# Products over a head's 64 channels on all 128 rows, in a two-layer hybrid decoder trunk

## The chip, the core and the metric

The kernel runs on one core of a Trainium2 chip. The metric is the device time of one execution in microseconds, the median of the runs. The kernel before takes 2547.66 us (median of 3 runs, 2547.12 to 2550.92). The engines are named as the profile names them: PE is TensorE's products and PEld its weight loads, DVE is VectorE, ACT ScalarE, POOL GpSimd, SP the engine that issues the transfers.

## The reference

Two layers over 256 tokens of 2048 channels, all in float32. A layer projects the normalized tokens once and hands the columns to three branches, whose results are gated and summed:

```python
h = rmsnorm(x, pre_norm[i])
pa, pb, pc, pg = split(h @ w_in[i])
y_a = mamba2_branch(pa, ...)      # state space, 16 heads of 64 channels
y_b = rwkv7_branch(pb, ...)       # delta rule, 16 heads of 64 channels
y_c = dsa_branch(pc, ...)         # sparse attention, 16 heads of 64 channels
merged = sum of sigmoid(gate_i) * (y_i @ w_branch_i)
x = x + rmsnorm(merged @ w_out[i], post_norm[i])
```

Three places contract over the 64 channels of one head. In branch B a low-rank product of 64 (decay and a) and, for each head, the Gram products of keys and key directions with key directions and receptances, 128 tokens at a time. In branch C the index scores (each of 16 index heads' queries with one shared key) and the attention logits:

```python
logits_idx = einsum('bqhd,bsd->bqhs', iqb, ik)          # 64 channels
score = einsum('bqh,bqhs->bqs', iwb, relu(logits_idx))  # then the top 64 keys of each query
logits = einsum('bqgrd,bqkgd->bqgrk', qg, ks)           # 64 channels
```

## The kernel before

Products that have to be exact to about float32 are made of two parts. An operand is split into a high part (rounded to `float32r`, which PE takes in one pass) and a low part (the rest), and a product is high x high + high x low + low x high. Over 128 channels that is three products (`acc`). Over a head's 64 channels the kernel has two helpers that need only two products. `stack` puts the high part of an operand on the head's 64 partitions and its low part on the other 64. `twice` puts the high part of the other operand on both halves and its low part into a separate tile, on the head's own half alone. `acc2` then issues a product over all 128 rows (high x high and low x high in one), and a second one over the head's 64 rows only (high x low):

```python
def acc2(self, out, w, x, lo, h, first=True, last=True):
    hs = self.HALF[h]
    self.mm(out, w, x, first, False)
    self.mm(out, w[hs], lo[hs], False, last)
```

`acc2` is called in `rwkv_prep` (the low-rank products, 2 for each of 8 channel blocks, and in `gram` 8 for each), in `index_scores` (one for each of 16 heads) and in `attend` (2 for each of 8 blocks). In the last two it takes the second 128 tokens' queries with all 256 keys. The first 128 tokens, which see 128 keys, take a plain float32 product there, `self.mm(pl[:, 0:128], ...)`, over 64 rows. A plain float32 product appears in the profile as two records.

Around this, weights stream through SP into `wraw`, ACT rounds them to `whi`, DVE (now and then POOL) subtracts to `wlo`, 512 columns at a time, and PE runs three products of 128x256 for each block of weights into a `psg` bank. Work of the branches is written as generators that are advanced between the products (`pump`), and its results lie in `psa` banks. Nothing is issued in the order in which it is written: every instruction is noted, and `Program.issue` replays them on a cost model of the core, giving each engine its most pressing ready instruction. All instructions are therefore issued from one line, L418. Each engine then runs its own list in order. The model's cost of a product depends on its type and columns; it has no term for the number of rows.

A layer runs the projections in the order `BCBBBBCCCCBBBBCCCCBBBBCCCCBBBBCAAAAAAAAAAAA`, then 48 merge steps (`c`, `b`, `a`, 16 each), then the output projection. Layer 1 has its merge from about 808 to 1249 us, layer 2 from about 2072 to 2503 us.

Of the kernel before, what the change touches and what calls it, by code (L numbers as in the profile page):

```python
# [37 lines left out]
# rotary order of a head's 64 channels: both of a pair lie in one quadrant of 32 partitions  # L38
# [8 lines left out]
def in_blocks():  # L47
    """Columns of w_in by block of 128 (-1 pads with zeros)."""
    ar = np.arange
    b = {}  # L50
# [21 lines left out]
# a layer's projections: units of two blocks, and the order in which the branches take turns  # L72
# [12 lines left out]
def plan():  # L85
    """The order in which a layer's weights come: (kind, which), in chunks of 128 x 1024."""
    p = []
    at = {k: iter(u) for k, u in UNITS.items()}
    for b in ORDER:
        u = next(at[b])  # L90
        p += [("cv", None)] if u == "cv" else [("br", w[1:]) if w[0] == "br" else ("in", w) for w in u]
    p += [("out", q) for q in range(4)]
    return p
# [14 lines left out]
def consts():  # L108
# [9 lines left out]
    # rows 8 i + q of a unit matrix, on the partitions 16 q to 16 q + 15  # L118
# [5 lines left out]
def pack(inp):  # L124
    """Layout of the inputs for the chip: copies only."""
# [77 lines left out]
class Program:  # L203
    """A sequential program of instructions, issued in the order in which a model of the core would run them.

    Instructions are noted as the trunk calls for them. issue() then gives each engine, whenever it is free, the most
    pressing instruction whose operands are there, so that no engine's queue waits on a result that comes late."""

# [21 lines left out]
    def tile(self, t, tag, bufs):  # L230
        """A tile of a tag takes one of its slots from its first access to its last."""
        of = self.tags.setdefault(tag, (bufs, []))
        assert of[0] == bufs
        self.tiles[t.tensor.name] = [tag, len(of[1]), 0, 0.0]
        of[1].append(t.tensor.name)
        return t

    @staticmethod
    def region(ap):
        """Partitions and columns that an operand may touch."""  # L240
# [14 lines left out]
    def note(self, eng, op, f, a, k):  # L255
# [6 lines left out]
        for aps, writes in ((r, False), (w, True)):  # L262
            for ap in aps:
# [8 lines left out]
                if writes or ap.space == bass.MemoryType.PSUM:  # L272
                    # of two engines that read a bank, one waits for the other
# [15 lines left out]
    def cost(eng, op, out, r, k):  # L289
        """Time on the engine, and after that until the result is there."""  # L290
# [24 lines left out]
    def issue(self, tc):  # L315
# [14 lines left out]
        # slots: of each tag, the tiles that are not yet dead, in order  # L330
# [102 lines left out]
urgent = ranked(0)      # frees the products' banks  # L433
critical = ranked(-1)   # all else waits for it
# [4 lines left out]
class Trunk:  # L439
# [66 lines left out]
    def rsqrt(self, x):  # L506
        """x (SBUF, > 0) -> x ** -0.5 in a new tile, to float32's accuracy."""
# [4 lines left out]
        # a first guess from the exponent, then y (15 - 10 x y^2 + 3 (x y^2)^2) / 8 (3/8 of it left out),  # L512
        # then y (3 - x y^2) / 2 (with that 3/8 put in)
# [24 lines left out]

    def rope_tables(self):
        """cos and signed sin of positions * frequency, reduced to a turn exactly by 12-bit parts."""  # L540
# [16 lines left out]
        # 1/(2 pi) = 0.15915494309189533576888376337251436...  # L557
# [20 lines left out]
        for dst, off in ((self.sin, 0.0), (self.cos, 0.25)):  # L578
# [4 lines left out]
            # a turn's fraction in [-1/2, 1/2]; the margin keeps the product within the table's range  # L583
# [31 lines left out]
    def fetch(self):  # L615
        """Load the next 128 x 1024 of weights."""
        l, n = divmod(self.nraw, self.wst.shape[1])
        if l < NL:
            # a layer's last ones come early, in room that the branches have left
# [6 lines left out]
    def prepare(self):  # L626
        """Weights of the products ahead, 128 x 512 at a time, each as an exact sum of two parts of 12 bits."""
        self.prog.rank, was = 1, self.prog.rank
        while len(self.ready) <= LA and (self.raw or self.nraw < NL * self.wst.shape[1]):
# [17 lines left out]
            # the last ones of a layer are kept for a second use, as quarters  # L647
# [18 lines left out]
    def parts(self, a):  # L666
        """a [128, 256] as (high, low)"""
# [5 lines left out]
    # Products over 64 channels, two at a time: the other 64 partitions add the low part's.  # L673
    HALF = (slice(0, 64), slice(64, 128))

    def stack(self, p, a, h):
        """p: on half h of the partitions the high part of a, on the other half the low part."""
# [4 lines left out]
    def twice(self, p, lo, a, h):  # L682
        """p: on both halves the high part of a, which lies on half h; lo, there: the low part."""
# [5 lines left out]
    def acc2(self, out, w, x, lo, h, first=True, last=True):  # L689
        """out += w.T @ x, w from stack, x and lo from twice."""  # L690
        hs = self.HALF[h]
        self.mm(out, w, x, first, False)
        self.mm(out, w[hs], lo[hs], False, last)

    def total(self, out, sel, x, first=True, last=True):
        """Sums over the partitions that sel (zeros and ones) names."""
# [4 lines left out]
    def acc(self, out, w, x, first, last):  # L701
        """out += w.T @ x, w and x as (high, low)."""
# [4 lines left out]
    def block(self, l, out, x, nch):  # L707
        """out [128, S] = a block of 128 columns of weights times x (pair of [128, 8 nch, S])."""
# [15 lines left out]
    def split(self, src, hi, lo, scale=None):  # L724
        """hi + lo = src (times a power of two), exactly."""
# [8 lines left out]
    def residual(self, src):  # L734
        """The residual stream, tokens on partitions: two tiles [128, DM]."""
# [6 lines left out]
    def square(self, ss, x):  # L742
        """ss [128, 1] = sum of squares of x [128, n] / DM"""
        self.s.activation(self.t2(512)[:, :x.shape[1]], x, AF.Square, scale=DM ** -0.5, accum_out=ss)

    def rstd(self, ss):
# [3 lines left out]
        # as rsqrt, in fewer steps  # L750
# [9 lines left out]
    def sums(self, n):  # L760
        """Room for n parts of a mean square, and 1e-6."""
# [5 lines left out]
    def prenorm(self, x, ss, u):  # L767
        """h as (high, low), channels on partitions."""
# [3 lines left out]
        # u: room for the scaled tokens  # L772
# [25 lines left out]
    def rope(self, outs, x, n):  # L798
        """x [P, n, S] (PSUM or SBUF) rotated, into each of outs."""
# [11 lines left out]
    def silu2(self, out, x_ps):  # L811
        """2 * silu(x)"""
# [10 lines left out]
    def misc_work(self, m1):  # L823
        v, s = self.v, self.s
        yield
        # index key: layer norm over its 64 channels, then rotary
# [19 lines left out]
        # tokens onto partitions  # L846
# [10 lines left out]
        # softplus(x) = max(x, 0) + log1p(u), u = exp(-|x|); log1p(u) = 2 atanh(u / (2 + u))  # L857
# [26 lines left out]
        # rows of it for all partitions to read  # L884
# [12 lines left out]
    @urgent  # L897
    def mix(self, x_ps, i):
        """Token shift: x (1 - mu) + mu x[t - 1]"""
# [5 lines left out]
    def rwkv_lora(self, x_ps):  # L905
        t = self.mix(x_ps, 0)
        self.s.activation(t[0:64], t[0:64], AF.Tanh)
        self.tw = [self.t1(dt=F32R) for _ in range(3)]
        for h in range(2):
            self.twice(self.tw[h], self.tw[2], t[self.HALF[h]], h)  # L910

    def rwkv_prep(self, Q, j, rm, km, vm):
# [14 lines left out]
        for h, p in enumerate((pl0, pl1)):  # L927
            self.stack(w2[:, h, :], w2r[self.HALF[h]], h)
            self.acc2(p[:, :S], w2[:, h, :], self.tw[h], self.tw[2], h)
# [6 lines left out]
        # normalized key direction  # L936
# [4 lines left out]
        # log decay = -KAP (1 + thw); its running sum per chunk, measured from the chunk's middle  # L941
# [13 lines left out]
        # k2 = k (1 + (a - 1) k_a), a = (1 + al) / 2  # L955
# [9 lines left out]
        # of a chunk: key directions for the deltas, receptances for the outputs  # L965
# [8 lines left out]
        # bonus  # L974
# [5 lines left out]
        As = [[self.t1(dt=F32R).rearrange("p (a t) -> p a t", a=2) for _ in range(3)] for _ in range(2)]  # L980
        for c in range(2):
            for h in range(2):
                self.twice(As[c][h], As[c][2], AR[c][self.HALF[h]], h)
# [594 lines left out]
```

## Time and profile before

| what | value |
|---|---|
| median of 3 runs | 2547.66 us (2547.12 to 2550.92) |
| profiled execution, span from first to last instruction | 2533.4 us |
| PE busy | 2447.7 us, 97% |
| DVE, ACT, POOL busy | 69%, 54%, 42% |
| mean granted clock of PE | 0.982 |
| moved by DMA | 407.71 MB, 161 GB/s |

The profiled execution's own time isn't listed apart from its span; the span is 14.3 us below the median of the runs. In the rows, `psg` is a bank of the large products, `psa` a bank of the branches', `t` any of the ring's tiles, `hh` and `hl` the high and low parts of the normalized tokens. A form such as 64\*128 is rows x columns of PE that a product uses, and the size behind it what it streams. A timeline's row merges neighbours with the same names: its start is the first one's, its length runs to the last one's end, and its form is the first one's.

### The profile page before, as it was taken

The page shows a single profiled execution, that of the slowest core. Times are in us where ns is not written, and L with a number is a line of the kernel's source. Part 1 is how long each engine was busy: PE and PEld are TensorE (multiplying, and loading weights), DVE is VectorE, ACT ScalarE, POOL GpSimd, SP SyncE. Part 2 cuts the span into 40 slices and gives each one's busy share as a digit, 9 for nine tenths or more (in the row PEclk, how much of TensorE's full clock was granted, in tenths as well). Part 3 has the DMA queues.
Part 4 walks back from the last instruction along what each step waited for, and adds up shares of the span by engine and source line. Part 5 has one row for each costly group of instructions (what it writes and reads, how often), then busy time and mean ns, then how long its engine had stood idle before and what let it go on. Part 6 is the DMA issues. An engine that isn't in the chain of part 4 may idle for free.

```text
span 2533.4 us, 50627 instructions
## 1 busy us (share of the span) xinstructions
PE 2447.7 (97%) x18750; PEld 2250.0 (89%) x18750; DVE 1750.5 (69%) x3466; ACT 1374.8 (54%) x2882; POOL 1059.9 (42%) x1726
## 2 busy tenths in 40 slices
PE   8999999999999999999989999999999999999998
PEld 7878888888889999999888888888888899999987
DVE  8856787678987565556576676786779865655565
ACT  6745555656544554545566554565565445544453
POOL 2556776577851000101134586686777500100001
PEclk9999999999999999999999998999999999999999
DMA  5363453625634565555543634536364445755563
GB/s 192 135 147 125 132 165 111 150 100 159 180 127 152 188 234 195 189 188 201 192 138 135 156 134 133 147 127 151 113 161 156 136 158 187 244 183 186 189 209 134
DMA packets 175192, 407.71 MB, mean 161 GB/s; under 512 B 73504, under 2 KB 76512, under 8 KB 173664
## 3 DMA queue, kind: packets, MB, share of 16 engines
q1 hardware_dynamic: 174944, 404.48, 50.6%
q8 instruction: 147, 2.41, 0.4%
q14 instruction: 101, 0.83, 0.1%
HBM read 395.99 MB, written 8.42 MB: 160 GB/s over the span
## 4 chain that ended last, share of the span: by engine, by line
PE 78%; DVE 9%; POOL 6%; issue 3%; DMA 3%; ACT 1%; SPq 0%; POOLq 0%; DVEq 0%; ACTq 0%
PE psg L418 65%; PE psa L418 13%; POOL t L418 6%; DVE t L418 5%; DVE wlo L418 3%; DMA d<-diag 1%; DMA wraw<-in_wst 1%; ACT t L418 1%; ACT whi L418 0%; DVE yb L418 0%; DMA t<-diag 0%; DVE n_x L418 0%; DMA yb<-in_x 0%; POOL ya L418 0%; SPq L418 0%
## 5 line engine op out<-in xcount | busy, mean ns | idle before, releaser
L418 DVE TENSOR_TENSOR wlo<-wraw,whi 128x512 fp32r<-128x512 f32 x1352 | 1023.7, 759 | 612.0 <-ACT whi L418 579.5
L418 ACT ACTIVATE whi<-wraw 128x512 fp32r<-128x512 f32 x1361 | 855.8, 631 | 831.0 <-PE psg L418 745.7
L418 PE MATMUL psg<-hh,wlo 128*128 128x256 f32 x4224 | 1206.3, 286 | 4.6 <-DVE wlo L418 4.3
L418 PE MATMUL psg<-hh,whi 128*128 128x256 f32 x4224 | 1207.8, 286 | 0.0
L418 PE MATMUL psg<-hl,whi 128*128 128x256 f32 x4224 | 1202.3, 285 | 1.0 <-DVE hl L418 1.0
L418 PEld LDWEIGHTS psg<-hh,wlo 128*128 128x128 f32 x4224 | 803.7, 190 | 20.3 <-DVE wlo L418 7.0
L418 PEld LDWEIGHTS psg<-hh,whi 128*128 128x128 f32 x4224 | 805.0, 191 | 14.8 <-issue 7.1
L418 PEld LDWEIGHTS psg<-hl,whi 128*128 128x128 f32 x4224 | 804.8, 191 | 14.2 <-issue 5.7
L418 POOL TENSOR_TENSOR t<-t,t 64x256 fp32r<-64x256 f32 (+30 forms) x822 | 547.2, 672 | 360.9 <-ACT t L418 253.0
L418 POOL TENSOR_TENSOR b_nm<-b_nm,t 128x256 f32<-128x256 f32 x64 | 48.6, 759 | 664.8 <-DVE t L418 657.1
L418 POOL TENSOR_TENSOR t<-t,d 128x63 f32<-128x63 f32 (+42 forms) x504 | 257.9, 513 | 62.8 <-DMA d<-diag 22.0
L418 PE MATMUL psg<-t,whi 128*128 128x256 f32 x1536 | 282.3, 283 | 0.0
L418 PEld LDWEIGHTS psg<-t,whi 128*128 128x128 f32 x1536 | 239.2, 191 | 0.9 <-issue 0.5
L418 ACT ACTIVATE t<-t 64x256 fp32r<-64x256 f32 (+4 forms) x420 | 173.8, 418 | 91.7 <-DVE t L418 75.8
L418 PE MATMUL psg<-t,wlo 128*128 128x256 f32 x768 | 217.6, 283 | 0.0
L418 PE MATMUL psa<-t,t 128*64 128x128 f32 (+4 forms) x800 | 191.6, 338 | 12.1 <-ACT t L418 6.4
L418 PEld LDWEIGHTS psa<-t,t 128*64 128x64 f32 (+2 forms) x800 | 112.4, 168 | 71.3 <-ACT t L418 8.2
L418 PEld LDWEIGHTS psg<-t,wlo 128*128 128x128 f32 x768 | 147.1, 192 | 0.4 <-issue 0.2
L418 ACT ACTIVATE t<-psa 128x256 f32<-128x256 f32 (+4 forms) x206 | 79.7, 396 | 105.7 <-PE psa L418 102.7
L418 PE MATMUL psg<-whi,hh 128*128 128x512 f32 (+1 forms) x268 | 98.5, 368 | 0.0
L418 PE MATMUL psg<-wlo,hh 128*128 128x512 f32 (+1 forms) x268 | 97.9, 365 | 0.0
L418 PE MATMUL psg<-whi,hl 128*128 128x512 f32 (+1 forms) x268 | 97.2, 365 | 0.0
(236 smaller groups left out, 2227.2 us busy)
## 6 DMA issues: line engine op xcount, KB each, us to landing
wraw<-in_wst SPq DMA_DIRECT2D x688, 512.0 KB, 3.3
d<-diag SPq DMA_DIRECT2D x64, 128.0 KB, 6.3
d<-diag SPq DMA_DIRECT2D x64, 64.0 KB, 5.4
t<-diag SPq DMA_DIRECT2D x16, 256.0 KB, 4.3
d<-in_wst SPq DMA_DIRECT2D x8, 512.0 KB, 4.6
ya<-in_x SPq DMA_DIRECT2D x8, 256.0 KB, 4.8
yb<-in_x SPq DMA_DIRECT2D x8, 256.0 KB, 6.2
t<-in_cst SPq DMA_DIRECT2D x8, 256.0 KB, 3.7
```

Of the source, the lines that this page charges most:

```text
L418: ops[i][2](*ops[i][3], **ops[i][4])
```

## The change

The low part is given 128 rows. A new tile `zl` holds 14 slots of 256 columns, set to zero once by POOL; `twice` writes a low part onto the head's half of a slot, and the other half stays zero. `acc2` then names all rows for both products. The low part of the index key already lay on both halves, where the 64 rows of the stack's low part now meet it too. The first tokens' float32 products in `index_scores` and `attend` become calls of `acc2` on 128 columns. For that the stacks hold all 256 tokens: `index_scores` makes a stack of its own for each head, just before its products, where it made two for four heads; `attend` has one tile for each head instead of one for both. The DMA scratch is reduced, which makes room for `zl`. Comments are left out of the new file.

```diff
+        self.zl = self.T([128, 14, S], "zl", dt=F32R)
+        self.g.memset(self.zl.bitcast(F32), 0.0)
...
-    def acc2(self, out, w, x, lo, h, first=True, last=True):
-        hs = self.HALF[h]
+    def acc2(self, out, w, x, lo, first=True, last=True):
         self.mm(out, w, x, first, False)
-        self.mm(out, w[hs], lo[hs], False, last)
+        self.mm(out, w, lo, False, last)
...
-        self.tw = [self.t1(dt=F32R) for _ in range(3)]
+        self.tw = [self.t1(dt=F32R) for _ in range(2)]
         for h in range(2):
-            self.twice(self.tw[h], self.tw[2], t[self.HALF[h]], h)
+            self.twice(self.tw[h], self.zl[:, 8 + h, :], t[self.HALF[h]], h)
...
-        As = [[self.t1(dt=F32R).rearrange("p (a t) -> p a t", a=2) for _ in range(3)] for _ in range(2)]
+        As = [[self.t1(dt=F32R).rearrange("p (a t) -> p a t", a=2) for _ in range(2)] for _ in range(2)]
+        Al = [[self.zl[:, 4 * jj + 2 * c + h, :].rearrange("p (a t) -> p a t", a=2) for h in range(2)] for c in range(2)]
...
-                    self.acc2(pG[:, c], M[h][:, ts], As[c][h], As[c][2], h)
+                    self.acc2(pG[:, c], M[h][:, ts], As[c][h], Al[c][h])
...
     def index_scores(self, iq, n):
-        iqs = [self.t1(dt=F32R).rearrange("p (c t) -> p c t", c=2) for _ in range(2)]
-        for h in range(2):
-            self.stack(iqs[h], iq[self.HALF[h], :, 128:256], h)
         for h in range(4):
-            yield
             hd = 4 * n + h
-            hs = slice(64 * (h % 2), 64 * (h % 2) + 64)
+            iqs = self.t1(dt=F32R)
+            self.stack(iqs, iq[self.HALF[h % 2], h // 2, :], h % 2)
+            yield
             pl = self.P()
-            self.mm(pl[:, 0:128], iq[hs, h // 2, 0:128], self.ik[hs, 0, 0:128])
-            self.acc2(pl[:, 128:384], iqs[h % 2][:, h // 2, :], self.iks[0], self.iks[1], h % 2)
+            self.acc2(pl[:, 0:128], iqs[:, 0:128], *[a[:, 0:128] for a in self.iks])
+            self.acc2(pl[:, 128:384], iqs[:, 128:256], *self.iks)
...
     def attend(self, j, q):
-        qs = self.t1(dt=F32R).rearrange("p (h t) -> p h t", h=2)
+        qs = [self.t1(dt=F32R) for _ in range(2)]
         for h in range(2):
-            self.stack(qs[:, h, :], q[self.HALF[h], 128:256], h)
+            self.stack(qs[h], q[self.HALF[h]], h)
...
-            self.mm(pl[:, 0:128], q[hs, 0:128], self.ck[hs, gp, 0:128])
-            self.acc2(pl[:, 128:384], qs[:, hb, :], self.cks[gp][hb], self.cks[gp][2], hb)
+            ks = self.cks[gp][hb], self.zl[:, 10 + 2 * gp + hb, :]
+            self.acc2(pl[:, 0:128], qs[hb][:, 0:128], *[a[:, 0:128] for a in ks])
+            self.acc2(pl[:, 128:384], qs[hb][:, 128:256], *ks)
...
-    nc = _bacc.Bacc("TRN2", target_bir_lowering=False, num_devices=1)
+    nc = _bacc.Bacc("TRN2", target_bir_lowering=False, num_devices=1, dynamic_dma_scratch_size=1024)
```

The order of issue is computed anew from the changed instructions. Three places show it. In a row stands what is written, then what streams and what is loaded as weights; the number at the end of a name tells tiles apart.

PE, second block pair of the index scores in layer 1, before: `ik` is the float32 product of the first tokens, `t_120` and `t_121` are the index key's high and low parts.

```order
1053 L418 MATMUL psg_487<-hl_102,whi_498 128x256
1054 L418 MATMUL psg_487<-hh_101,wlo_499 128x256
1055 L418 MATMUL psa_509<-ik_171,t_422_484 128x128
1056 L418 MATMUL psa_500<-t_120_182,t_430_492 128x256
1057 L418 MATMUL psa_500<-t_121_183,t_430_492 128x256
1058 L418 MATMUL psa_509<-t_120_182,t_430_492 128x256
1059 L418 MATMUL psa_509<-t_121_183,t_430_492 128x256
1060 L418 MATMUL psg_487<-hh_101,whi_502 128x256
```

The same place after the change:

```order
1069 L418 MATMUL psg_483<-hh_102,whi_499 128x256
1070 L418 MATMUL psa_501<-t_120_182,t_436_498 128x128
1071 L418 MATMUL psa_501<-t_121_183,t_436_498 128x128
1072 L418 MATMUL psa_501<-t_120_182,t_436_498 128x256
1073 L418 MATMUL psa_501<-t_121_183,t_436_498 128x256
1074 L418 MATMUL psg_483<-hl_103,whi_499 128x256
1075 L418 MATMUL psg_483<-hh_102,wlo_500 128x256
1076 L418 MATMUL psg_483<-hh_102,whi_505 128x256
```

A head's four products, all split parts, now stand together, and each head waits for its own stack.

POOL, the stacks of the same block pair, before: the first row is the end of the rotary, the next two are the stacks' low parts, and `t<-t,d` and `t<-t,t` in small sizes are the inverse of branch B.

```order
86 L418 TENSOR_TENSOR t_422_484<-t_423_485,t_424_486 128x512
87 L418 TENSOR_TENSOR t_429_491<-t_422_484,t_429_491 64x256
88 L418 TENSOR_TENSOR t_430_492<-t_422_484,t_430_492 64x256
89 L418 TENSOR_TENSOR t_379_441<-t_378_440,d_376_438 128x63
90 L418 TENSOR_TENSOR t_378_440<-t_379_441,t_378_440 128x63
```

After:

```order
89 L418 TENSOR_TENSOR t_418_480<-t_419_481,t_420_482 128x512
90 L418 TENSOR_TENSOR t_425_487<-t_418_480,t_425_487 64x256
91 L418 TENSOR_TENSOR t_430_492<-t_418_480,t_430_492 64x256
92 L418 TENSOR_TENSOR t_436_498<-t_418_480,t_436_498 64x256
93 L418 TENSOR_TENSOR t_441_503<-t_418_480,t_441_503 64x256
94 L418 TENSOR_TENSOR t_373_435<-t_372_434,d_370_432 128x63
```

Four low parts of stacks stand ahead of the inverse where two stood.

POOL, the program's start after the change: `n_s` and `b_cu` are small cells, and `wlo` is the low part of the first weights. Before, the same rows stood there without the third.

```order
6 L418 MEMSET n_s_65 128x1
7 L418 MEMSET n_s_66 128x1
8 L418 MEMSET zl_80 128x3584
9 L418 MEMSET b_cu_277 128x2
10 L418 MEMSET b_cu_369 128x2
12 L418 TENSOR_TENSOR wlo_85<-wraw_82,whi_84 128x512
```

The zeros are set ahead of the first weights' low parts.

## Rows read from the trace of the kernel before

**Rows 1.** The page's head: span, busy time of each engine with its share and number of instructions, PE's granted clock in tenths over 40 slices of the span, and the shares of the chain that ended last by engine.

```profile
span 2533.4 us, 50627 instructions
PE 2447.7 (97%) x18750; PEld 2250.0 (89%) x18750; DVE 1750.5 (69%) x3466; ACT 1374.8 (54%) x2882; POOL 1059.9 (42%) x1726
...
PE 78%; DVE 9%; POOL 6%; issue 3%; DMA 3%; ACT 1%; SPq 0%; POOLq 0%; DVEq 0%; ACTq 0%
```

**Rows 2.** Who waited for whom over the whole span: the engine and the tile that it was about to write, what released it, then total us, times, longest us.

```profile
ACT whi L418 <- PE psg L418: 745.7, 961, 6.8
...
DVE wlo L418 <- ACT whi L418: 579.5, 772, 6.8
...
PEld psa L418 <- POOL t L418: 36.7, 40, 4.5
...
PE psa L418 <- POOL t L418: 28.3, 27, 4.3
```

**Rows 3.** Busy time by stage: the stretch, its length, then PE, PEld, DVE, ACT and POOL with the number of instructions, PE's granted clock, the share of DMA and GB/s.

```profile
160.00:300.00 140.00, 128.98 (x896) 113.46 (x895) 83.75 (x145) 72.38 (x158) 98.75 (x158) 0.93 0.43 128
300.00:500.00 200.00, 193.76 (x1451) 168.88 (x1449) 149.35 (x361) 112.43 (x271) 132.82 (x239) 1.00 0.54 144
808.00:1249.00 441.00, 441.00 (x3439) 427.64 (x3438) 264.28 (x420) 229.92 (x415) 38.70 (x55) 1.00 0.58 199
```

**Rows 4.** Groups of PE's instructions by tiles and form: records, busy us, mean ns of one, idle time before them. The first is the low products, the second the full ones beside them, the third and fourth the float32 products of the first tokens (index scores, then logits).

```profile
L418 PE MATMUL psa<-t,t 64*128 64x256 f32 x224 | 81.6, 378 | 4.5 <-POOL t L418 4.2
...
L418 PE MATMUL psa<-t,t 128*128 128x256 f32 x224 | 75.6, 343 | 4.4 <-ACT t L418 4.1 <-POOL t L418 0.3
...
L418 PE MATMUL psa<-t,ya 64*128 64x128 f32 x64 | 14.2, 315 | 0.0
...
L418 PE MATMUL psa<-ik,t 64*128 64x128 f32 x64 | 11.8, 338 | 7.0 <-POOL t L418 6.9
```

**Rows 5.** Timeline of PE around one low product among plain ones: start in us from the span's start, length, then what. The row at 274.39 is a low product and the full product of the next pair.

```profile
273.72 0.28 PE L418 MATMUL psg<-hh,wlo 128*128 128x256 f32 x1
...
274.18 0.28 PE L418 MATMUL psg<-hh,whi 128*128 128x256 f32 x1
274.39 0.69 PE L418 MATMUL psa<-t,t 64*128 64x256 f32 x2
274.92 0.28 PE L418 MATMUL psg<-hl,whi 128*128 128x256 f32 x1
275.04 0.28 PE L418 MATMUL psg<-hh,wlo 128*128 128x256 f32 x1
```

**Rows 6.** Timeline of PE, two pieces in the index scores. The row at 287.08 is two pairs of a full and a low product, and the row behind it a float32 product's two records; at 291.30 such a product stands apart, ahead of two pairs.

```profile
287.08 1.22 PE L418 MATMUL psa<-t,t 128*128 128x256 f32 x4
288.14 0.38 PE L418 MATMUL psa<-ik,t 64*128 64x128 f32 x2
288.44 0.39 PE L418 MATMUL psg<-hh,wlo 128*128 128x256 f32 x1
288.67 0.28 PE L418 MATMUL psg<-hh,whi 128*128 128x256 f32 x1
...
291.09 0.28 PE L418 MATMUL psg<-hh,wlo 128*128 128x256 f32 x1
291.30 0.48 PE L418 MATMUL psa<-ik,t 64*128 64x128 f32 x2
291.71 1.46 PE L418 MATMUL psa<-t,t 128*128 128x256 f32 x4
```

**Rows 7.** Busy time in short stretches around two falls of the granted clock, columns as in rows 3.

```profile
289.30:292.70 3.40, 3.40 (x18) 2.24 (x16) 2.18 (x4) 1.76 (x4) 3.32 (x9) 1.00 0.44 154
292.70:299.50 6.80, 6.80 (x29) 5.24 (x29) 1.76 (x6) 2.02 (x5) 3.42 (x5) 0.50 0.08 20
...
1545.40:1548.80 3.40, 3.40 (x13) 2.06 (x12) 0.00 (x0) 1.41 (x5) 1.38 (x4) 1.00 0.02 5
1548.80:1559.00 10.20, 10.20 (x42) 8.19 (x43) 5.22 (x9) 2.79 (x6) 5.04 (x8) 0.50 0.16 51
```

**Rows 8.** Groups of ACT's and POOL's instructions by form, columns as in rows 4: halves of stacks and of `twice` with 256 columns, and those of the logits' stacks with 128.

```profile
L418 POOL TENSOR_TENSOR t<-t,t 64x256 fp32r<-64x256 f32 x156 | 140.1, 898 | 87.9 <-ACT t L418 46.8 <-issue 31.9 <-POOL t L418 1.7
...
L418 POOL TENSOR_TENSOR t<-ya,t 64x128 fp32r<-64x128 f32 x32 | 17.7, 552 | 24.7 <-ACT t L418 22.8
...
L418 ACT ACTIVATE t<-t 64x256 fp32r<-64x256 f32 x232 | 96.0, 414 | 34.0 <-DVE t L418 20.6 <-POOL t L418 9.1
...
L418 ACT ACTIVATE t<-ya 64x128 fp32r<-64x128 f32 x32 | 9.8, 306 | 2.7 <-POOL ya L418 2.2
```

**Rows 9.** Timeline of POOL at the start, with the idle time ahead of an instruction in brackets.

```profile
13.79 2.79 POOL L418 TENSOR_TENSOR wlo<-wraw,whi 128x512 fp32r<-128x512 f32 x2 [12.79 <-DVE whi L418]
```

**Rows 10.** The chain that ended last within two stretches, 160 to 300 us and 300 to 500 us: shares by engine and tile.

```profile
by line: PE psg L418 40.2%; PE psa L418 19.1%; DMA d<-diag 12.3%; DVE t L418 8.9%; POOL t L418 8.6%; issue 5.1%; DVE wlo L418 4.1%; ACT t L418 1.5%; ACT whi L418 0.9%; DVE b_sc L418 0.2%; POOLq L418 0.1%; ACTq L418 0.0%
...
by line: PE psg L418 40.7%; PE psa L418 21.3%; POOL t L418 10.4%; DVE t L418 7.8%; issue 5.3%; DMA d<-diag 4.0%; DMA wraw<-in_wst 3.2%; DVE wlo L418 3.0%; DMA diag<-t 1.4%; ACT t L418 1.1%; POOL ya L418 0.6%; ACT whi L418 0.6%; DVE yb L418 
```

**Rows 11.** Timeline of PE in the logits: a full and a low product of one head, then the float32 product's two records of the other.

```profile
477.94 0.58 PE L418 MATMUL psa<-t,t 128*128 128x256 f32 x2
478.14 0.48 PE L418 MATMUL psa<-t,ya 64*128 64x128 f32 x2
478.56 0.70 PE L418 MATMUL psa<-t,t 128*128 128x256 f32 x2
```

More of the change, by code (lines that the diff above doesn't have):

```diff
@@ L928, in rwkv_prep @@
             self.stack(w2[:, h, :], w2r[self.HALF[h]], h)
-            self.acc2(p[:, :S], w2[:, h, :], self.tw[h], self.tw[2], h)
+            self.acc2(p[:, :S], w2[:, h, :], self.tw[h], self.zl[:, 8 + h, :])
         thw, al = self.t1(), self.t1()
@@ L979, in rwkv_prep @@
                 self.stack(m[h], M[self.HALF[h]], h)
-        As = [[self.t1(dt=F32R).rearrange("p (a t) -> p a t", a=2) for _ in range(3)] for _ in range(2)]
+        As = [[self.t1(dt=F32R).rearrange("p (a t) -> p a t", a=2) for _ in range(2)] for _ in range(2)]
+        Al = [[self.zl[:, 4 * jj + 2 * c + h, :].rearrange("p (a t) -> p a t", a=2) for h in range(2)] for c in range(2)]
         for c in range(2):
             for h in range(2):
-                self.twice(As[c][h], As[c][2], AR[c][self.HALF[h]], h)
+                self.twice(As[c][h], Al[c][h], AR[c][self.HALF[h]], h)
         yield
@@ L1192, in index_scores @@
             yield
-        iqs = [self.t1(dt=F32R).rearrange("p (c t) -> p c t", c=2) for _ in range(2)]
-        for h in range(2):
-            self.stack(iqs[h], iq[self.HALF[h], :, 128:256], h)
         for h in range(4):
+            hd = 4 * n + h
+            iqs = self.t1(dt=F32R)
+            self.stack(iqs, iq[self.HALF[h % 2], h // 2, :], h % 2)
             yield
-            hd = 4 * n + h
-            hs = slice(64 * (h % 2), 64 * (h % 2) + 64)
             pl = self.P()
-            self.mm(pl[:, 0:128], iq[hs, h // 2, 0:128], self.ik[hs, 0, 0:128])
-            self.acc2(pl[:, 128:384], iqs[h % 2][:, h // 2, :], self.iks[0], self.iks[1], h % 2)
+            self.acc2(pl[:, 0:128], iqs[:, 0:128], *[a[:, 0:128] for a in self.iks])
+            self.acc2(pl[:, 128:384], iqs[:, 128:256], *self.iks)
             rl = self.t2(384)
@@ L1277, in proj_c @@
         self.rope([self.ck], p, 2)
-        self.cks = [[self.t1(dt=F32R) for _ in range(3)] for _ in range(2)]
+        self.cks = [[self.t1(dt=F32R) for _ in range(2)] for _ in range(2)]
         for i in range(2):
             for b in range(2):
-                self.twice(self.cks[i][b], self.cks[i][2], self.ck[self.HALF[b], i, :], b)
+                self.twice(self.cks[i][b], self.zl[:, 10 + 2 * i + b, :], self.ck[self.HALF[b], i, :], b)
         yield
```

## The prediction

> **What bounds the kernel.** I read the page first: TensorE (PE) is busy 97% of the span and holds 78% of the chain that ended last; no other engine is over 69% [rows 1]. A busy PE is not a PE at its peak, so I then asked who waits for whom. The waits say that the preparers of weights stand behind PE: ACT waits 745.7 us for the products to give its buffers back, and DVE 579.5 us for ACT in turn, while PE's own named waits, those for POOL, are 28.3 us, and its weight loads' 36.7 [rows 2]. The stages split the span in two kinds. In the merge (808 to 1249, and again in the second layer) PE runs 3439 products in 441 us, 0.128 us each, and nothing the change touches stands there. In the branch stages it is still busy over 90% of the time, yet one product takes 0.138 us (1451 in 200 us) to 0.156 (896 in 140) [rows 3]. So there PE is held by something that counts as busy, and that is where to look.
>
> **What the touched products cost now.** Four groups matter: 224 full products of a head's pair, 224 low products that read 64 rows alone, and 128 records of fp32 products on 64 rows [rows 4]. An fp32 product leaves two records, so these are 64 products: 2 layers times 16 heads, for the index scores and for the logits. The timeline then shows the price, read by starts, since ends are modelled. Plain products start every 0.115 us (273.72 to 274.18 is four steps, 0.46 us). Where one 64-row product stands among them, the four products from 274.18 to 275.04 take 0.86 us: 0.40 more, with no wait named [rows 5]. In the first piece of the next group the stretch from 287.08 to 288.67 holds two pairs, a fp32 product's two records right behind the second low product, and one plain product: 7 records in 1.59 us, against 7 x 0.115 = 0.81, so 0.78 for two trips into 64 rows and back, 0.39 each [rows 6]. The fp32 records that follow a low product cost no trip of their own. I take **0.39 us for each trip** from 128 rows to 64 and back. It isn't accumulation into one bank: the plain products accumulate too.
>
> **The change part by part.**
> Low products on all rows: there are at least 224 trips (every fp32 product beside a low one, as at 288.14) and at most 288 (every one apart, as at 291.30) [rows 6]. Seeing both, I take the middle, 256. All of them go, since after the change hi, low and first-token products all name 128 rows: 256 x 0.39 = **100 us** off PE (87 to 112). The low product itself costs a plain 0.115 before and after. Products on 64 rows elsewhere (the blocks' solves) stay.
>
> First tokens by split parts: 64 products of two fp32 records become 64 pairs of 128 columns, so the number of records stays. No row shows a split product that narrow. Below it is half a 256-column one, 0.06 us; above, if such a narrow one ran at the fp32 rate, a whole fp32 product, 0.23 (two records at 0.115). 128 products at 0.06 to 0.23 are 7.7 to 29.4 us, against 128 x 0.115 = 14.7 now: 7 us less to 15 more. I take 0.115 each, **nothing**, as the weight load of 128 columns is the same beside any number of columns.
>
> TensorE's clock: in two stretches dense with trips the granted clock fell from 1.00 (2.4 GHz) to 0.50 (1.2 GHz) though PE counts as busy throughout: 18 products in the 3.40 us before 292.7 and 13 in the 3.40 before 1548.8, where plain work has 29; the slow stretches are 6.8 and 10.2 us [rows 7]. Half of 17.0 is 8.5 us; without the trips more products stand there, so I count **8** (0 to 8.5). The Trainium skill ("TensorE: Matmul & The Clock Gate", "Why this matters for your kernels") ties a lost clock to gaps in which the engine idles; by that rule alone this term is nothing and the time 6 us later; the trace differs, its engine was busy.
>
> Stacks: index scores take a stack of 256 columns for each head, 4 for a block pair where there were 2 (of 2 x 128); over 8 block pairs that is 16 more on ACT and on POOL. The 32 stacks of the logits grow from 128 to 256 columns. POOL: 16 x 0.898 + 32 x (0.898 - 0.552) = 25.4 us; ACT: 16 x 0.414 + 32 x (0.414 - 0.306) = 10.1 [rows 8]. Both lie beside PE: ACT is busy 72 of 140 us in the stage of the index scores, POOL 99 of 140 [rows 3]. I cost them at nothing; if the cover goes, it is PE that waits for a stack, at most 25 us.
>
> The memset of the zeros, 128 x 3584, stands on POOL ahead of its first low parts. POOL sits idle for the 12.79 us up to 13.79 [rows 9]; a 128x512 subtraction takes 1.40 there, so seven such widths, 9.8 us, are the upper bound and still fit. Nothing. Tiles: three `t1` a pair of `twice` become two, which only loosens the ring.
>
> **What of it reaches the end.** 108 us come off PE, but off the end only where the chain is on PE; where PE waits for POOL or DVE, a faster PE just waits longer. In 160 to 300 us the chain is on PE for 59%, in 300 to 500 for 62% [rows 10]. By that average some 65 us would arrive, and all 108 if the chain always ran through these products. They stand in thick clusters in which PE has no gap (the 3.40 of 3.40 in [rows 7]), so nearer the top: I take 0.8. What is late next is POOL's stacks and inverse and DVE's vector work, which hold most of the rest of the chain there. 108 x 0.8 = **86 us**. The span of the profiled execution is 2533.4, 14.3 below the median of 2547.66; I take what lies around it as unchanged and subtract from the median: 2547.66 - 86 = **2462**.
>
> **Rivals.**
> (a) *Less passes on.* The order of issue is planned for a PE without trips, so other engines should keep up; but if the stage's 35 to 40% of chain off PE grows with each microsecond taken from PE, only 0.4 arrives: 43 us, 2505. For it: POOL is busy 3/4 of 160 to 300. Against it: ACT's and DVE's waits on PE.
> (b) *PE waits for the stacks, and it is slower.* A head's index products now need a stack begun one step ahead, on a POOL that also runs the inverses in small operations. 32 index heads and 32 logit heads each waiting w us cost 64 w; from w = 1.35 the 86 us are gone, and at 2 us the time is 2547.66 - 86 + 128 = 2590. Waits for POOL of about 0.9 us (36.7 us of loads) exist [rows 2], but the sum of all of them is less than half of what it takes.
> (c) *Side by side.* From 477.94 to 478.56 stand a full product, a low one, and the two records of a fp32 product that reads the other 64 rows: four records and a trip, 4 x 0.115 + 0.39 = 0.85 us by the prices above. They take 0.62, two records' worth less [rows 11], so here the low product and a fp32 record ran beside one another. If 64-row products generally ran beside one another for nothing, the change would add 224 x 0.115 = 26 us, 2573. The Trainium skill ("TensorEngine Tiling (Array Packing)", "When to Use Tiling") advises row tiling for a contraction of 64 or less, which speaks against the change. In the pieces read the low products stand among products of 128 rows [rows 5, 6], and the 0.39 us is measured there.
> (d) *The 0.39 isn't the row count* but something the new low products keep (another tile, another bank): nothing changes but the stacks, 2548. Against it: plain products that change bank, such as those around 274, show no gap.
>
> **Chances.** Forecast with its own spread (gains of 60 to 113 us) 0.72; (a) 0.19; (b) 0.03; (c) 0.02; (d) 0.04. The likeliest gives 2462. Low end: 112 + 8.5 + 7 less work at a share of 0.87 is 111 us, 2437. High end: into (a), a gain of 40, 2508. Outside stay (b), (c), (d), the worse part of (a) and a little below: about 2 in 10. About 0.2% (5 us) is what a measurement of this kernel can tell from no change: faster 0.92, same 0.04, slower 0.04.
>
> **What would show it.** In the changed profile: no PE group of 64 rows by 128 columns; 224 low products named after the zeros' tile with starts 0.115 us after the one before; the same number of PE records; branch stages near 0.125 to 0.13 us a product and the merge as now; fewer stretches at 0.50; PE's waits on POOL up by some tens of us. I would be wrong if the narrow split products start over 0.2 us apart, if the low products keep a gap, or if PE's waits grow by more than half of what its products lose.

## The result, and the profile after

The changed kernel takes **2486.14 us** (median of 4 runs, 2482.46 to 2487.15) against 2547.39 for the kernel before in the same comparison: a ratio of 0.9772, 95% interval 0.9749 to 0.9795, so 52 to 64 us faster. The forecast was 2462, range 2437 to 2508, faster. The direction and the range hold, and the gain is 61 us of the 86.

The page's head of the changed kernel, as in [rows 1]:

```profile
span 2485.1 us, 50696 instructions
PE 2373.2 (95%) x18750; PEld 2230.4 (90%) x18750; DVE 1765.5 (71%) x3466; ACT 1375.8 (55%) x2898; POOL 1110.3 (45%) x1743
...
PE 74%; DVE 12%; POOL 5%; issue 4%; DMA 3%; ACT 2%; SPq 0%; POOLq 0%; DVEq 0%; ACTq 0%
```

PE's records are as many as before. Its busy time fell by 74.5 us, and its idle time (span less busy) rose from 85.7 to 111.9: 26.2 of what PE gave up turned into waiting. The sum, 48.3 us, is the difference of the two spans. The chain moved from PE (78 to 74%) to DVE (9 to 12%).

The stages, columns as in [rows 3]:

```profile
160.00:300.00 140.00, 127.33 (x1003) 120.95 (x1002) 100.64 (x171) 79.97 (x175) 113.67 (x177) 0.96 0.52 147
300.00:500.00 200.00, 187.66 (x1471) 169.34 (x1469) 154.25 (x367) 117.09 (x282) 149.40 (x263) 0.96 0.54 146
808.00:1230.00 422.00, 422.00 (x3278) 408.64 (x3277) 244.95 (x378) 218.47 (x397) 44.40 (x60) 1.00 0.60 200
```

In 160 to 300 us PE now runs 1003 products where it ran 896, and DVE, ACT and POOL are fuller too. In 300 to 500 it is only 1471 for 1451: there its busy time fell and its clock with it (1.00 to 0.96). The merge keeps its pace, 0.129 us a product.

What the touched products cost now. First the groups (columns as in [rows 4]), then the timeline of PE at two places (start, length, what):

```profile
L418 PE MATMUL psa<-zl,t 128*128 128x256 f32 x192 | 52.9, 297 | 1.9 <-POOL zl L418 1.7
...
L418 PE MATMUL psa<-t,t 128*128 128x128 f32 x128 | 27.2, 275 | 13.0 <-POOL t L418 12.7
...
L418 PE MATMUL psa<-zl,t 128*128 128x128 f32 x32 | 8.8, 275 | 0.0
```

```profile
136.27 0.38 PE L418 MATMUL psa<-t,t 128*128 128x256 f32 x1
136.49 0.28 PE L418 MATMUL psa<-zl,t 128*128 128x256 f32 x1
136.61 0.28 PE L418 MATMUL psa<-t,t 128*128 128x256 f32 x1
136.73 0.28 PE L418 MATMUL psa<-zl,t 128*128 128x256 f32 x1
136.85 0.28 PE L418 MATMUL psg<-hl,whi 128*128 128x256 f32 x1
...
147.12 0.28 PE L418 MATMUL psg<-hh,whi 128*128 128x256 f32 x1
147.24 0.62 PE L418 MATMUL psa<-t,t 128*128 128x128 f32 x4
147.70 0.28 PE L418 MATMUL psg<-hl,whi 128*128 128x256 f32 x1
```

No form 64\*128 is left. Full and low products alternate every 0.12 us from 136.49 on, where a pair in [rows 6] lost 0.39. The row at 147.24 is an index head's four products, two of 128 columns and two of 256: 0.46 us in all, 0.115 each on average. The narrow split product costs what I took for it.

Who PE waits for, as in [rows 2]:

```profile
ACT whi L418 <- PE psg L418: 709.6, 922, 5.8
...
PE psa L418 <- DVE t L418: 25.7, 16, 4.5
PE psa L418 <- POOL t L418: 24.7, 26, 4.5
PE psa L418 <- ACT t L418: 22.3, 20, 2.7
```

Before, POOL's was 28.3 us [rows 2], and the other two were:

```profile
PE psa L418 <- DVE t L418: 16.2, 13, 2.5
PE psa L418 <- ACT t L418: 11.9, 13, 1.8
```

The new waiting is spread over DVE and ACT, and POOL's share fell.

### The profile page after: what moved, and what is told of

Read it like the earlier page. It is cut to its first block, busy times and chain, and to the rows that moved or that the text cites. A ratio compares the mean times of both kernels' runs of the same rounds, so it can differ in the third digit from the quotient of the medians.

```text
span 2485.1 us, 50696 instructions
## 1 busy us (share of the span) xinstructions
PE 2373.2 (95%) x18750; PEld 2230.4 (90%) x18750; DVE 1765.5 (71%) x3466; ACT 1375.8 (55%) x2898; POOL 1110.3 (45%) x1743
## 4 chain that ended last, share of the span: by engine, by line
PE 74%; DVE 12%; POOL 5%; issue 4%; DMA 3%; ACT 2%; SPq 0%; POOLq 0%; DVEq 0%; ACTq 0%
PE psg L418 63%; PE psa L418 11%; DVE t L418 6%; POOL t L418 4%; DVE wlo L418 4%; DMA wraw<-in_wst 2%; ACT t L418 1%; ACT whi L418 1%; DMA d<-diag 1%; POOL zl L418 1%; DVE yb L418 0%; DVE b_cu L418 0%; DMA yb<-in_x 0%; DVE n_x L418 0%; DMA b_ut<-diag 0%
## 5 line engine op out<-in xcount | busy, mean ns | idle before, releaser
L418 PEld LDWEIGHTS psg<-hh,wlo 128*128 128x128 f32 x4224 | 806.3, 191 | 16.3 <-DVE wlo L418 10.4
L418 POOL TENSOR_TENSOR t<-t,t 64x256 fp32r<-64x256 f32 (+30 forms) x762 | 499.1, 660 | 315.0 <-ACT t L418 220.2
L418 POOL TENSOR_TENSOR t<-t,d 128x132 f32<-128x132 f32 (+44 forms) x504 | 266.1, 530 | 63.1 <-DMA d<-diag 31.0
L418 ACT ACTIVATE t<-t 64x256 fp32r<-64x256 f32 (+5 forms) x436 | 179.6, 417 | 95.2 <-DVE t L418 79.8
L418 PE MATMUL psa<-t,t 128*64 128x128 f32 (+3 forms) x704 | 136.0, 305 | 23.2 <-POOL t L418 12.7
L418 PEld LDWEIGHTS psa<-t,t 128*128 128x128 f32 (+1 forms) x704 | 90.7, 169 | 44.6 <-POOL t L418 16.6
```

The costliest lines, as they stand in the source:

```text
L418: ops[i][2](*ops[i][3], **ops[i][4])
```

## The experiments

A run's time is a median of 4 runs; the kernel before is at 2540 to 2545 in each comparison. Of the executions I use the span and the mean granted clock; they stand in the table at the end of this section.

### What a trip costs, alone

Two kernels add 192 products that nothing reads to the changed kernel's merges, where PE has no gap. They differ in the partitions that the products read.

```diff
-            self.block(l, p[:, 0, :], h, 2)
-            self.block(l, p[:, 1, :], (yh, yl), 1)
+            for x, n, k in ((h, 2, 0), ((yh, yl), 1, 1)):
+                self.block(l, p[:, k, :], x, n)
+                self.mm(self.P()[:, 0:256], yh[0][0:64, 0:128], yh[1][0:64, 0:256])
```

> The changed kernel with 192 more products that nothing reads, two in each of the 96 merge steps, each alone among products of 128 rows: both operands are 64 partitions of the branch's split result, 256 columns. In the merge PE is the bound, so all of their time shows. Theory (0.115 us a product and 0.39 a trip): 192 x 0.505 = 97 us slower than the changed kernel, near 2583. If a 64-row product costs no more than another (rival d), 22 us slower, near 2508.

> The same 192 extra products at the same places, with 128 partitions of the same tiles as operands. Theory: 192 x 0.115 = 22 us slower than the changed kernel, near 2508. The difference between the 64-row probe and this one, over 192, is the price of one trip: 0.39 us by the theory, 0 by rival d.

Measured: 2582.95 us with 64 partitions, 2511.01 with 128 (`0:128` in the last line). The full products cost about (2511.01 - 2486.14) / 192 = 0.130 us each. **A trip costs (2582.95 - 2511.01) / 192 = 0.375 us.** The timeline shows it at the same product of both, first with 64 rows, then with 128:

```profile
851.70 0.28 PE L418 MATMUL psg<-hh,wlo 128*128 128x256 f32 x1
851.90 0.38 PE L418 MATMUL psa<-t,t 64*128 64x256 f32 x1
852.22 0.50 PE L418 MATMUL psg<-t,whi 128*128 128x256 f32 x2
852.56 0.28 PE L418 MATMUL psg<-t,wlo 128*128 128x256 f32 x1
```

```profile
852.13 0.28 PE L418 MATMUL psg<-hh,wlo 128*128 128x256 f32 x1
852.25 0.28 PE L418 MATMUL psa<-t,t 128*128 128x256 f32 x1
852.36 0.40 PE L418 MATMUL psg<-t,whi 128*128 128x256 f32 x2
852.60 0.28 PE L418 MATMUL psg<-t,wlo 128*128 128x256 f32 x1
```

Four products take 0.86 us there (851.70 to 852.56) and 0.47 here (852.13 to 852.60): 0.39, what I had read from [rows 5, 6]. The only difference is the rows, so rival (d) is out, and with it (c) for products that stand alone. The Trainium skill ("TensorEngine Tiling (Array Packing)", "Key Properties") says that a change of tiling mode drains TensorE; the runs are in line with that, at 0.375 us for a change to 64 rows and back.

### The two halves of the change

> Half of the change: the low products read 128 rows through the zeros' tile in all three places, but the first tokens' products stay plain fp32 on 64 rows and the stacks stay as before the change. 64 trips of 0.39 us remain (the fp32 products, two records each). Theory (the gain is trips taken off PE, 0.39 us each, of which about 0.6 reaches the end): 256 - 64 = 192 trips gone, 75 us off PE, so about 45 us faster than the kernel before, near 2502. If the stacks that grew are what ate the rest of the forecast (rival b): this one, without them, is as fast as the changed kernel or faster, 2486 or below.

```diff
-            self.acc2(pl[:, 0:128], iqs[:, 0:128], *[a[:, 0:128] for a in self.iks])
-            self.acc2(pl[:, 128:384], iqs[:, 128:256], *self.iks)
+            self.mm(pl[:, 0:128], iq[hs, h // 2, 0:128], self.ik[hs, 0, 0:128])
+            self.acc2(pl[:, 128:384], iqs[h % 2][:, h // 2, :], *self.iks)
...
-            self.acc2(pl[:, 0:128], qs[hb][:, 0:128], *[a[:, 0:128] for a in ks])
-            self.acc2(pl[:, 128:384], qs[hb][:, 128:256], *ks)
+            self.mm(pl[:, 0:128], q[hs, 0:128], self.ck[hs, gp, 0:128])
+            self.acc2(pl[:, 128:384], qs[:, hb, :], *ks)
```

Measured: 2479.43 us, against 2502 expected by trips alone. With the first tokens' float32 products back it is 7 us faster than the whole change.

> The changed kernel with the index scores' first tokens and stacks as before the change (32 fp32 products on 64 rows, two stacks for four heads, 16 stacks fewer on ACT and POOL), the logits as changed. If the stacks made head by head are what cost the changed kernel its last gain (rival b), this is 5 to 10 us faster than it, near 2479, although 32 trips (12 us of PE) come back. If the trips are worth more than the stacks: 5 us slower, near 2491.

Here only the index scores' part of that edit is made. Measured: 2489.19 us, 3 us slower than the whole change: the stacks of the index scores, which I had suspected, are worth less than the 32 trips that come back here, and are not what the 7 us come from.

> The other cut: branch C as in the changed kernel (index scores and logits on 128 rows, first tokens by split parts), but branch B's low products (low-rank and Gram, 160 of the 224) read 64 rows again. Theory of trips: about 96 of 256 trips gone, 37 us off PE, some 23 us faster than before, near 2524. If the cost of a trip depends on the place, or if the gain comes from the first tokens' fp32 products, it differs: all of the gain here would be 2486, none 2547.

```diff
-            self.acc2(p[:, :S], w2[:, h, :], self.tw[h], self.zl[:, 8 + h, :])
+            self.acc2(p[:, :S], w2[:, h, :], self.tw[h], self.zl[:, 8 + h, :], h=h)
...
-                    self.acc2(pG[:, c], M[h][:, ts], As[c][h], Al[c][h])
+                    self.acc2(pG[:, c], M[h][:, ts], As[c][h], Al[c][h], h=h)
```

(`acc2` with `h` takes `w[hs]` and `lo[hs]` for its low product, as before the change.) Measured: 2516.70 us, ratio 0.9895 to before (0.9855 to 0.9935), against 2524 expected. Both parts of the trips pay, neither alone.

### How much the order of issue decides

7 us could be the work's or the order's, since every edit makes the planner order everything anew. So I moved constants of the planner by a little, with the same work.

> The changed kernel with one constant of the planner moved a little (a product's time until its result is there, 200 to 206 ns), so that the order of issue differs in many small places and the work is the same. It tells how far the order alone moves the time. Theory that the order is second: within 5 us of 2486. If the order decides what passes on: 10 us or more off.

> The same with another constant (the time until a result is there for PE, 130 to 136 ns). Same expectations: within 5 us of 2486 if the order is second, 10 us or more off if not. Together with the other it says whether the 7 us by which the kernel with old first tokens was faster can be read as the work's.

```diff
-LP = 200
+LP = 206
```

```diff
-LT = 130
+LT = 136
```

Measured: 2503.31 and 2503.32 us, both 17 us slower than the changed kernel. The order alone is worth more than the 7 us in question, so the halves can't be told apart that finely by single kernels. Was the whole gain an order's luck? The same moves in the kernel before, and one in the half:

> The kernel before the change, planned with the moved constant (a product's time until its result is there, 200 to 206 ns). With the changed kernel the same move cost 17 us. If such moves cost the kernel before as much (the constants fit both equally well), it is near 2564, and the change is worth some 60 us under this plan too. If the kernel before does not care, near 2545, the change is worth about 42 us there, and some 18 of its 61 us are the luck of one order.

> The kernel before with the other moved constant (130 to 136 ns); the changed kernel with it is at 2503. Equal sensitivity: near 2564. None: near 2545. The three pairs (given constants, a, b) together are the estimate of what the change does apart from the order of issue.

> Half of the change (low products on 128 rows, first tokens' products and stacks as before it) with the moved constant. Under the given constants it was 7 us faster than the whole change, under this one the whole change is at 2503. If the old first tokens are really better: 5 to 10 us below 2503. If that 7 us was the order: above it, or equal.

Measured: 2572.73 and 2569.13 us for the kernel before, 2486.70 for the half. The change is worth 61, 69 and 66 us under the three plans: it is not luck. The half is faster than the whole by 7 and by 17. The two of a pair were mostly timed in different comparisons. By the ratios to the unmoved kernel before beside each, the change is worth 2.3, 3.0 and 2.8%, and the half is ahead by only 0.3% (7 us) and 0.35% (9 us) with intervals that overlap, so that the half is faster is not shown.

> The changed kernel, planned with what the trace shows of PE: 256 columns in 0.116 us instead of 0.108, and 0.195 us for each change between 64 and 128 rows or columns. The work is the same, the order is new. If the gain that did not arrive was lost because the planner thought PE faster than it is, so that other engines' work stood too late or too early in their lists, this is 10 us or more faster than 2486. If the other engines' own time is the limit there, within 5 us.

```diff
-                return n / 2.4 + 1.7, 0.0
+                return n / 2.2, 0.0
...
                 last = ops[i][8][0]
+                busy += 195.0 * (form != was)
+                was = form
```

Measured: 2584.01 us, 98 slower with the same work. What it lost, the waits show in part: PE stood longest for DVE (53.3 us, 25.7 in the changed kernel), and its weight loads, of the engines that the profile names, for ACT. Whether this plan's PE is truer is not shown: 0.195 us is half of a trip's 0.39, but no run measured what a change of columns costs, and the plan charges that too.

```profile
PE psa L422 <- DVE t L422: 53.3, 27, 6.2
PE psa L422 <- ACT t L422: 33.8, 31, 3.6
...
PEld psa L422 <- ACT t L422: 45.7, 52, 3.8
```

> Half of the change again, planned with a PE that is faster than the real one (256 columns in 0.104 us instead of 0.108). The plan with a slower, truer PE lost 98 us. If a plan that takes PE for faster than it is keeps PE fed (it brings the other engines' work forward), this is faster than 2479. If the given constant is a tuned optimum, some 10 to 20 us slower, like the other moves.

```diff
-                return n / 2.4 + 1.7, 0.0
+                return n / 2.5 + 1.7, 0.0
```

Measured: **2466.41 us** (2466.30 to 2469.98), ratio 0.9715 to before (0.9676 to 0.9753): the fastest of all, 20 us below the changed kernel and 13 below the same half under the given constants, though they were not timed in one comparison. By the ratios to before (0.9715, and 0.9745 for the half) it is 8 us ahead of the half, and the intervals overlap. One run in each direction is not enough to say why a plan that takes PE for faster is better; it is the same direction twice.

### Where the orders differ: the granted clock

Much of what separates these kernels is the mean granted clock. Multiplying it with the span takes out the pulses that were withheld, as if PE could have used every one (an upper bound, since it waits in some of those stretches; half a step of the clock's last digit is worth 1.3 us). Span, clock and product are those of the profiled execution; the last column is the mean of the product over all executions on record, 4 of a run and 21 of the kernel before.

| kernel | median us | span us | clock | span x clock | mean of all |
|---|---|---|---|---|---|
| before | 2547.39 | 2533.4 | 0.982 | 2488 | 2487 |
| before, constant a | 2572.73 | 2586.3 | 0.963 | 2491 | 2495 |
| before, constant b | 2569.13 | 2564.0 | 0.973 | 2495 | 2493 |
| changed | 2486.14 | 2485.1 | 0.980 | 2435 | 2436 |
| changed, a | 2503.31 | 2505.0 | 0.973 | 2437 | 2442 |
| changed, b | 2503.32 | 2502.4 | 0.975 | 2440 | 2442 |
| changed, old index scores | 2489.19 | 2488.2 | 0.981 | 2441 | 2443 |
| changed, other planner costs | 2584.01 | 2584.7 | 0.971 | 2510 | 2504 |
| low products only | 2479.43 | 2474.9 | 0.985 | 2438 | 2441 |
| low products only, a | 2486.70 | 2486.6 | 0.984 | 2447 | 2447 |
| low products only, faster PE | 2466.41 | 2464.6 | 0.988 | 2435 | 2435 |
| branch C only | 2516.70 | 2522.1 | 0.977 | 2464 | 2468 |
| probe, 64 rows | 2582.95 | 2579.9 | 0.984 | 2539 | 2535 |
| probe, 128 rows | 2511.01 | 2506.3 | 0.983 | 2464 | 2459 |

The three plans of the kernel before, 53 us apart in span, lie within 7 here; the three of the changed one, 20 apart, within 5; the probes' difference is 75 / 192 = 0.39 a trip. By the means over all executions the planner's moves cost 6 us of work in the changed kernel and 6 to 8 in the kernel before, so two thirds to three quarters of what they cost goes through the clock. The whole change does 5 us less work than its half under both plans (2436 and 2441; 2442 and 2447). That the half is faster is thus a matter of the clock (0.985 and 0.984 against 0.980 and 0.973); whether its fewer stacks or the order keep it up was not separated. The kernel with other planner costs is the exception: most of its loss is left without the clock (2504 against 2436).

The clock differs between executions of one program in one order as well. The 21 executions of the kernel before have spans of 2524.5 to 2554.9 us at clocks of 0.984 to 0.972, and products of 2482 to 2493. A comparison of two single executions can therefore not tell what a change does to the clock.

The halves' expectations come out right in this column. The low products alone save 2487 - 2441 = 46 us of work (45 expected) and branch C alone 2487 - 2468 = 19 (23 expected). What the first gained beyond that, its higher clock gave.

What PE did before the clock fell is seen in rows of before, constant a, and of the changed kernel, with columns as in [rows 3]:

```profile
300.00:500.00 200.00, 192.61 (x1299) 166.01 (x1298) 136.00 (x312) 98.37 (x235) 127.07 (x233) 0.87 0.43 122
...
370.00:376.66 6.66, 4.39 (x37) 4.06 (x35) 5.81 (x10) 2.88 (x7) 4.75 (x7) 1.00 0.70 186
376.66:410.79 34.13, 34.13 (x172) 26.40 (x172) 8.86 (x25) 9.18 (x22) 10.53 (x20) 0.50 0.21 65
```

```profile
480.90:485.80 4.90, 1.99 (x16) 1.56 (x15) 4.00 (x6) 2.66 (x6) 4.59 (x9) 1.00 0.32 103
485.80:492.60 6.80, 5.78 (x30) 5.26 (x29) 6.39 (x12) 1.89 (x4) 5.47 (x9) 0.50 0.46 123
```

In the first kernel the clock averages 0.87 over 200 us in which PE counts as busy for 192.61, and it gets through 1299 products where [rows 3] has 1451. Most of that is one stretch of 34.13 us at 0.50. It began after PE had waited 2.27 us for POOL, and it holds products of the blocks' solves (64\*64 and 128\*64) among full ones and none of the 64\*128 that the change touches, so it is no sign of what trips do to the clock. In the changed kernel the fall at 485.80 comes after PE was busy 1.99 of 4.90 us. It had waited, as at two other falls (idle time ahead and what ended it in brackets):

```profile
181.79 1.06 PE L418 MATMUL psa<-t,t 128*128 128x128 f32 x4 [3.51 <-POOL t L418]
...
485.07 0.39 PE L418 MATMUL psa<-t,blkr 128*128 128x256 f32 x1 [2.32 <-ACT t L418]
...
1404.83 0.48 PE L418 MATMUL psa<-t,t 128*128 128x128 f32 x1 [4.50 <-POOL t L418]
```

The whole traces say how far each goes. The trace of the kernel before has 13 stretches at 0.50. Ahead of 4 of them ([rows 7] shows two) PE counts as busy for at least 4.2 of the last 5 us, and 4 to 11 of its 23 to 25 products there are 64\*128. The trace of the changed kernel has 18 stretches, and ahead of each PE stands idle for at least 1.7 of the last 5 us. So the falls without a wait are gone with the trips, and falls after a wait are more. The other traces agree: 5 of 18 falls come that way in before, constant a, 6 of 19 under constant b, 2 of 18 with branch C only, and none where branch B's low products read all rows.

## Why the prediction was right in direction and too large in size

**The price of a trip: right.** 0.39 us read from starts in the timeline; 0.375 by the probes' medians and 0.39 by their spans with the clock taken out. The middle that I took for their number was near: counted in the order of PE's records, changes from 128 to 64 rows fell from 428 to 188, 240 trips. At 0.39 they are 94 us off PE, where I had 100.

**The narrow split products: right.** Four products of an index head take 0.46 us, 0.115 each; of the range 0.06 to 0.23 the middle holds.

**The memset: right, with room.** It took 3.08 us, under the bound of 9.8, on an idle POOL:

```profile
0.86 3.08 POOL L418 MEMSET zl<- 128x3584 f32 x1
```

**What reaches the end: the step that failed.** I took 0.8 of 108 us, arguing from the dense clusters against the chain's own average of 0.6 in [rows 10]. With the clock taken out the spans differ by 2488 - 2435 = 52 us (before rounding), 53 and 55 under the other two plans, and by 51 in the means over all executions: 0.54 to 0.59 of 94. The halves give 46 of 74 us (190 trips counted), 0.62, and 19 of 42 (107 trips), 0.46. So rival (a)'s mechanism was at work, over half of the way from my 0.8 to its 0.4: the chain's average over the stage came near the share, and the look of the places where the products stand did not. Where the rest went can be added up from the starts of PE's products in the two traces. Steps from one product to the next without idle time between them took 87 us less, and steps with idle time took 39 more (128 of them, where there were 86). The page's idle time shows only 26.2 of these 39, because the modelled length of a product covers the beginning of the wait behind it. Of the 94 us, 48 are the difference of the spans, 39 turned into steps with waits, and 7 aren't accounted for.

**The clock term: right in sign, and the profiled pair hides it.** I counted 8 us back from stretches in which trips had brought the granted clock down [rows 7]. The two profiled executions say the opposite: the mean clock went from 0.982 to 0.980, which is 45.6 us withheld in 2533.4 and 49.7 in 2485.1, 4 us lost. But the profiled execution of before was one of its better ones. Over all executions the mean clock is 0.979 before and 0.981 after, 53.5 us withheld and 47.2: 6 us won. Under the other two plans it is 19 and 14 us. That dense trips were a cause rests on the falls without a wait counted above, which are there in every trace that keeps branch B's trips and in no other; the 192 single trips of the probe brought none. PE also gets to the end of its work sooner now, waits for DVE, ACT or POOL for 1 to 4.5 us, and the clock falls there (at 485.80 in the rows above), which takes part of that back. The rule of the Trainium skill that I weighed ("TensorE: Matmul & The Clock Gate", "Why this matters for your kernels": idle gaps cost the clock) fits these falls; at the 4 falls of before the rows differ, since PE was busy there.

**Rival (b), waits for the stacks: there, but small.** The first tokens' products wait 12.7 us for POOL in all (the group x128 above, 96 of them first tokens'); before, the fp32 product of the index scores waited 6.9 [rows 4]. PE's waits on POOL as a whole did not rise by tens of us as I wrote; they fell from 28.3 to 24.7, and DVE's and ACT's rose by 9.5 and 10.4. Old index scores in the changed kernel brought nothing.

**The signs: not all came.** No group of 64\*128, as many records, and the merge as before came as named. The branch stages run at 0.136 to 0.140 us a product (1471 in 200, 1003 in 140), above the 0.125 to 0.13 that I named; stretches at 0.50 are 18 instead of 13. The low products of 256 columns named after `zl` are 192 and not 224, since the index key's low part has a tile of its own.

**What lies around the span: wrong.** I took the 14.3 us between span and median as a fixed part. The changed kernel's profiled execution took 2487.15 us around a span of 2485.1, so only 2 us lie around it. If as much lay around the span before, the execution that was profiled was some 12 us faster than the median; the kernel before ran between 2526 and 2557 in these comparisons. The spans differ by 48.3 us, the medians by 61.

The sum with measured terms, as means over all executions: 51 us less work (0.54 of 94) and 6 from the clock are 57, the difference of the mean spans (2540.5 and 2483.4). The 61 of the first comparison has 4 more, since the kernel before stood at 2547.39 there and at 2540 to 2545 in the later ones. The 0.54 is read from these same executions, so this is an account of the gain and no second proof of the share; the halves give a second reading.

## What to carry to other kernels

A product on half of the rows, alone in a stream of products on all rows, cost 0.38 to 0.39 us here on top of its own 0.12 to 0.13; zeros in the other half were cheaper than the change of form. Look for this in starts, not in busy time, which hides it.

What the faster step on the bounding engine brought to the end was near the chain's share on that engine in that stage (0.46 to 0.62 of what was taken off PE, where the chain stood at 0.59 and 0.62), not more, and a kernel whose order is planned needs two or three plans of both versions before a difference of 10 us is called the work's. Compare spans times granted clock beside the times, over several executions: it told work from clock here, and a single pair got the clock's part wrong.

## What the runs showed that I had not expected

Moves of 3 to 5% in one planner constant cost 17 us in the changed kernel and 29 to 33 in the kernel before (against the unmoved one beside it), with the same instructions, and most of it through PE's granted clock (0.963 to 0.982 for the same work before, 0.973 to 0.980 after). The clock fell to 0.50 both after waits of PE of 2 to 4.5 us and, before the change, in stretches in which PE counts as busy but changes between 64 and 128 rows.

A planner that was told a slower PE, for plain products the real pace (0.116 us for 256 columns instead of 0.108, and 0.195 a change of form), made the changed kernel 98 us slower; one that took PE for faster than it is (0.104) made the fastest, with the half of the change.
